# MLP tokens taken without their norm, and every first product by seven

## The chip, the cores and the metric

The program runs on one core of one Trainium2 chip. Its time is device microseconds of that core. The kernel before takes 1178.8 us, the median of three runs (1178.77 to 1179.98). Five engines work side by side: TensorE (PE in the profile; its weight loads are PEld), VectorE (DVE), ScalarE (ACT), GpSimd (POOL) and SyncE (SP), which here only issues DMAs.

## The reference

A trunk of two layers over 512 tokens of width 1024, in float32. Layer 0 mixes the tokens by two groups of attention heads, layer 1 by neighbourhood attention; both are followed by the same kind of MLP, and the change is in the MLPs and at their borders.

```python
def rmsnorm(x, g):
    y = x * rsqrt(mean(x * x, axis=-1, keepdims=True) + EPS)
    return y * g
def sq_relu_mlp(h, w_up, w_down):          # w_up 1024 x 4096, w_down 4096 x 1024
    u = relu(h @ w_up)
    return (u * u) @ w_down
for layer in range(2):
    h = h + attention(rmsnorm(h, norm_mix[layer])) @ w_out
    h = h + sq_relu_mlp(rmsnorm(h, norm_ffn[layer]), w_up[layer], w_down[layer])
return rmsnorm(h, final_norm)
```

For one token the norm is a single factor r, and r squared is 1/v with v = mean(x * x) + EPS. Since relu(r a) = r relu(a) for a positive r, the MLP of the normed token is 1/v times the MLP of the token that is only multiplied by the gain g. So h + mlp = (h v + mlp without the norm) / v.

## The kernel before, in words

**Layout and precision.** The residual hT lies transposed: eight tiles of 128 channels x 512 tokens. Every product is done on float32 split into a high part (rounded by ScalarE to the matmul's type) and a low part (the rest, by VectorE), by three matmuls: high x high, high x low, low x high. `split` (L827) and `split_g` (L510) do this for tokens, `chunk` (L183) for plain weights.

**Plain and by seven.** A plain step (`mm3`, L505) is three matmuls of 512 columns for one k tile of 128 and one tile of 128 outputs. `Seven` (L314) is a product of two output tiles and two k tiles at a time in which the tokens are halved (2 x 256), and seven products of half the width take the place of eight. It needs sums of weights: `seven_chunk` (L295) loads 2 x 128 x 256 weights and makes four extra blocks with three POOL instructions (L302 to L304), then ScalarE (L308) and VectorE (L309) split the 896 columns. It needs sums of tokens: `Seven.sums` (L331) makes them with POOL or VectorE, `Seven.split` (L344) splits the seven pieces per pair of k tiles into high (ScalarE, L363) and low (VectorE, L364). `Seven.run` (L381) issues 4 x 7 x 3 matmuls of 256 columns for one group of two output tiles of the first product (L393 to L395), then evacuates four banks by one ScalarE copy and four VectorE additions (L401 to L405).

**The MLP** (`mlp`, L1249). The 4096 hidden channels are 32 tiles, and they are made and used in stages: SIZES gives, for each layer, how many tiles each stage makes and uses by the plain second product; the numbers behind the third are tiles which the second product takes by seven, and in layer 1 the last four are kept for the end, which is done with tokens on partitions (`down`, L1663). `first_product` (L1109) makes the tiles. Before, its first six tiles were plain: x is split with the gain by `split_g`, the squares are added up by VectorE (`sumsq_acc`, L517), a column sum gives r by three Newton steps (`compact_r`, L524), r is broadcast over partitions by four transposes (`bcast_cols`, L532), and the evacuation multiplies by it. From then on the tokens times r are summed for the sevens (`x_sums`) and split piece by piece beside the first stage's second product (`later`). The other 26 tiles come by seven. The second product adds into hT (L1264), the part by seven too (L1303).

**What surrounds it.** In front of the MLP stands the rest of the output projection: four of eight k tiles in layer 0, three in layer 1 (`out_proj`, L926), in two groups of four output tiles, with weights in chunks of two k tiles x 512. Behind layer 0's MLP the sums are split into layer 1's tokens and `valuesC` (L1380) starts on them. Behind layer 1's, hT is transposed (`turn`, L1656) and added to the last product (`add`, L1594).

**What sets the order.** Weights are planned in the order of the program; `weights` (L237) keeps five chunks on the way and two split ahead; the split ones lie in rings of three buffers, raw ones in a ring of four or in a free slot out of thirty (`Slot`), which the tokens and hidden tiles use as well. The issue order of each engine is made by a planner that takes the instructions in program order and may put a ready one ahead of one that waits; within `fixed_order` (L956: layer 1's attention) the written order holds for TensorE, ScalarE, VectorE and POOL.

## Time and profile before

| what | before |
|---|---|
| median of three runs | 1178.8 us |
| the profiled execution | 1179.44 us |
| its span | 1177.7 us |
| granted TensorE clock | 0.998 |
| TensorE busy | 1160.4 us, 99% |
| VectorE, ScalarE, POOL busy | 892.0, 644.5, 536.2 us |

The span is the time from the first to the last instruction of the profiled execution; about 1.7 us lie around it. Busy shares are over the whole span. TensorE's matmuls overlap in the records, so a single duration (0.39 us for 512 columns) is longer than the distance from one start to the next; stage lengths divided by counts tell the pace. In rows of groups, the arrow names what was written and read, `x` the count, then follow the busy time, the mean in ns, and the idle time in front of it.

### The profile page before, as it was taken

To read this page: it belongs to the slowest core of one execution; us is meant where nothing else is said; L and a number is where in the kernel's file an instruction comes from. 1 tells how busy PE (TensorE), PEld (TensorE's weight loads), DVE (VectorE), ACT (ScalarE), POOL (GpSimd) and SP (SyncE) were. 2 spreads that over 40 slices of the span, in tenths; PEclk is the share of its full clock that TensorE was granted. 3 is DMA by queue.
4 is the path that set the end of the run, shared out by engine and by line. 5 is a ranking of instruction groups with operands and counts; after the bars stand their busy time and mean duration, and the time that the engine had idled before them with its cause. 6 is when DMAs were issued, how large, how long until landed. Compare 5 with 4: busy or idle time off the path is not lost. (4 is left out here: it accounts for less than half of the span.)

```text
span 1177.7 us, 20031 instructions
## 1 busy us (share of the span) xinstructions
PE 1160.4 (99%) x7212; PEld 1023.8 (87%) x7212; DVE 892.0 (76%) x1530; ACT 644.5 (55%) x1097; POOL 536.2 (46%) x683
## 2 busy tenths in 40 slices
PE   9999999999999999999999999999999999999997
PEld 8667788888898999989998998988889899998996
DVE  5588998878875588798884676667987677779775
ACT  4577676764444366743453555555553356663344
POOL 3256252315452878429802232221357458724920
PEclk9999999999999999999999999999999999999999
DMA  7223315222425523225226564433243223232322
GB/s 246 73 59 92 86 54 135 72 63 81 154 83 178 190 78 95 89 89 162 72 73 174 126 177 132 128 106 116 90 153 108 81 72 94 89 130 75 126 73 72
DMA packets 111235, 128.04 MB, mean 109 GB/s; under 512 B 9139, under 2 KB 88928, under 8 KB 111136
## 3 DMA queue, kind: packets, MB, share of 16 engines
q1 hardware_dynamic: 108080, 119.30, 33.2%
q0 software_dynamic: 2304, 6.31, 2.3%
q8 instruction: 57, 0.93, 0.3%
q10 hardware_dynamic: 752, 1.15, 0.3%
q14 instruction: 42, 0.34, 0.1%
HBM read 104.32 MB, written 6.29 MB: 94 GB/s over the span
## 5 line engine op out<-in xcount | busy, mean ns | idle before, releaser
L309 DVE TENSOR_TENSOR wlo<-a,whi 128x896 fp32r<-128x896 f32 x133 | 165.8, 1251 | 75.0 <-ACT whi L308 72.5
L308 ACT ACTIVATE whi<-a 128x896 fp32r<-128x896 f32 x133 | 125.8, 949 | 159.3 <-PE s L394 36.7
L506 PE MATMUL mm<-a,whi 128*128 128x512 f32 x473 | 190.3, 405 | 0.6 <-ACT a L832 0.3
L507 PE MATMUL mm<-a,whi 128*128 128x512 f32 x473 | 187.2, 396 | 0.1
L508 PE MATMUL mm<-a,wlo 128*128 128x512 f32 x473 | 186.2, 395 | 0.0
L202 DVE TENSOR_TENSOR wlo<-raw,whi 128x1024 fp32r<-128x1024 f32 (+4 forms) x113 | 132.1, 1172 | 56.0 <-ACT whi L212 55.9
L302 POOL TENSOR_TENSOR a<-a 128x128 f32<-128x128 f32 x133 | 89.6, 674 | 146.6 <-DMA a<-in_ffn_w_up_dram 80.5
L212 ACT ACTIVATE whi<-raw 128x1024 fp32r<-128x1024 f32 (+3 forms) x116 | 112.0, 967 | 75.4 <-PE o L507 17.7
L303 POOL TENSOR_TENSOR a<-a 128x256 f32<-128x256 f32 x133 | 119.0, 895 | 10.4
L304 POOL TENSOR_TENSOR a<-a 128x128 f32<-128x128 f32 x133 | 115.7, 870 | 10.4
L395 PE MATMUL mm<-a,wlo 128*128 128x256 f32 x390 | 110.3, 283 | 1.1 <-DVE wlo L309 1.1
L393 PE MATMUL mm<-a,whi 128*128 128x256 f32 x390 | 109.9, 282 | 0.0
L394 PE MATMUL mm<-a,whi 128*128 128x256 f32 x390 | 109.9, 282 | 0.0
L508 PEld LDWEIGHTS mm<-a,wlo 128*128 128x128 f32 x473 | 88.7, 188 | 21.2 <-issue 1.7
L506 PEld LDWEIGHTS mm<-a,whi 128*128 128x128 f32 x473 | 88.8, 188 | 20.2 <-issue 1.5
L507 PEld LDWEIGHTS mm<-a,whi 128*128 128x128 f32 x473 | 89.1, 188 | 18.7 <-issue 1.7
L1004 POOL TENSOR_SCALAR p<-p,ti 128x512 f32<-128x512 f32 x64 | 46.1, 722 | 87.0 <-DVE ti L1003 70.2
L1438 POOL TENSOR_SCALAR p<-p,ti 128x256 f32<-128x256 f32 x64 | 35.4, 564 | 105.0 <-DVE ti L1437 92.0
L393 PE MATMUL t<-a,whi 128*128 128x256 f32 x280 | 79.0, 282 | 0.0
L394 PE MATMUL t<-a,whi 128*128 128x256 f32 x280 | 78.8, 282 | 0.0
L395 PE MATMUL t<-a,wlo 128*128 128x256 f32 x280 | 78.8, 281 | 0.0
L395 PEld LDWEIGHTS mm<-a,wlo 128*128 128x128 f32 x390 | 73.6, 189 | 1.9 <-DVE wlo L309 1.9
(336 smaller groups left out, 3255.3 us busy)
## 6 DMA issues: line engine op xcount, KB each, us to landing
a<-in_ffn_w_up_dram SPq DMA_DIRECT2D x100, 256.0 KB
raw<-in_ffn_w_down_dram SPq DMA_DIRECT2D x42, 512.0 KB
a<-in_ffn_w_down_dram SPq DMA_DIRECT2D x33, 256.0 KB
raw<-in_od_w_qkv_dram SPq DMA_DIRECT2D x64, 128.0 KB
raw<-in_ffn_w_up_dram SPq DMA_DIRECT2D x12, 512.0 KB
raw<-in_ev_w_in_dram SPq DMA_DIRECT2D x12, 384.0 KB
a<-a SPq DMA_DIRECT2D x18, 256.0 KB
bias<-bx SPq DMA_DIRECT2D x16, 256.0 KB
```

What stands on the lines that cost most here:

```text
L202: z = lambda: (eng or DVE).tensor_tensor(to, src, f32(high), op=ALU.subtract)
L212: ACT.activation(hi[:, 0:m], raw[:, 0:m], AF.Copy)
L303: POOL.tensor_tensor(r[:, 4:6], r[:, 2:3].to_broadcast([P, 2, P]), r[:, 0:7:6], op=ALU.add)
L304: POOL.tensor_tensor(r[:, 7], r[:, 3], r[:, 5], op=ALU.subtract)
L308: ACT.activation(hi[:, 0:896], raw[:, 128:1024], AF.Copy)
L309: DVE.tensor_tensor(lo[:, 0:896], raw[:, 128:1024], f32(hi[:, 0:896]), op=ALU.subtract)
L393: PE.matmul(o, wh, x[:, 0], start=kp == 0 and n in (0, 1, 3, 5), stop=False, skip_group_check=True)
L394: PE.matmul(o, wh, x[:, 1], start=False, stop=False, skip_group_check=True)
L395: PE.matmul(o, wl, x[:, 0], start=False, stop=kp == self.np - 1, skip_group_check=True)
L506: PE.matmul(o, wh, xh, start=first, stop=False)
L507: PE.matmul(o, wh, xl, start=False, stop=False)
L508: PE.matmul(o, wl, xh, start=False, stop=last)
```

## The change

1. The first product takes x times the gain, without r. `tokens(kp)` makes the scaled copy of two k tiles on ScalarE, their sums on POOL (the last pair's on VectorE) and the split pieces, all ahead of the first product.
2. All 32 hidden tiles come by seven; plain tiles, `x_sums`, `later` and the evacuation with r go. SIZES becomes (12, 8, 12) and (10, 8, 10, 4): two plain second products a layer instead of three.
3. The rest of the output projection is done in four pairs of output tiles, with chunks of all its k tiles x 256 and k innermost; after each pair its tokens are taken.
4. `norm` is now a list of 19 steps beside the first stage's second product: eight squares with their additions, v by column sums and its reciprocal, two broadcasts (v and 1/v), and eight multiplications of hT by v. The bias table's DMAs follow in the same stage.
5. The last evacuation of each pair adds into hT and then multiplies by 1/v, a second VectorE instruction of 128 x 1024. In layer 1 the last product's additions take 1/v as a factor.

```diff
-    SIZES = (6, 6, 8, 12), (6, 4, 8, 10, 4)
+    SIZES = (12, 8, 12), (10, 8, 10, 4)
...
+        def tokens(kp):
             raw = Slot(F32)
             for z in range(2):
                 k = 2 * kp + z
-                DVE.scalar_tensor_tensor(raw.t[:, S * z : S * z + S], hT[:, k, :], gffn(l, k), rb, op0=ALU.mult,
-                                         op1=ALU.mult)
-            for _ in x7.sums(kp, raw):
+                ACT.activation(raw.t[:, S * z : S * z + S], hT[:, k, :], AF.Copy, scale=gffn(l, k))
+
+            for _ in x7.sums(kp, raw, DVE if kp == KD // 2 - 1 else POOL):
                 pass
+            for _ in x7.split(kp):
+                pass
+
+        def norm():
+
+            acc = pp.tile([P, S], F32, tag="p", name=nm("acc"))
+            for k in range(KD):
+                sumsq_acc(k, acc, DVE)
+                yield
+            free_bank = mmb if flip[0] else stb
+            b = free_bank()
+            for i in range(4):
+                PE.matmul(b[:, i : i + 1], acc[:, i * P : (i + 1) * P], ones[:, 0:1], start=True, stop=True)
+            v, rc, rb = keep([P, 4], F32, "v"), keep([P, 4], F32, "rc"), keep([P, S], F32, "rb")
+            DVE.tensor_scalar(v, b[:, 0:4], 1.0 / D, EPS, op0=ALU.mult, op1=ALU.add)
+            DVE.reciprocal(rc, v)
+            hold["rc"], hold["rb"] = rc, rb
+            yield
+            for col, to in ((v, acc), (rc, rb)):
+                bk = free_bank()
+                bcast_cols(lambda i: col[:, i : i + 1].to_broadcast([P, P]), P, bk)
+                ACT.activation(to, bk, AF.Copy)
+                yield
+            for k in range(KD):
+                DVE.tensor_tensor(hT[:, k, :], hT[:, k, :], acc, op=ALU.mult)
+                yield
...
-    def mlp(l, last=None):
+    def mlp(l, w_o, k0, last=None):
+        ok = [s_.pair() for s_ in O[k0:]]
+        pairs = [out_proj(w_o, k0, ok, [2 * kp, 2 * kp + 1], lambda n, kp=kp: [mmb(), sbk() if kp % 2 else mmb()])
+                 for kp in range(KD // 2)]
+        tokens, stage, ahead, norm = first_product(l)
+        ahead()
+        flip[0] = 0
+        for kp, gen in enumerate(pairs):
+            for _ in gen:
+                pass
+            tokens(kp)
...
             for c, gen in enumerate(gens):
                 for i, _ in enumerate(gen):
                     if z == 0:
-                        later(c, i)
-                    elif z == 1:
-                        next(bias, None)
-                        if i % 3 == 0:
+                        steps = steps or norm()
+
+                        if i not in (8, 9, 10, 12, 13):
+                            next(steps, None)
+                        if c or i > 24:
                             next(bias, None)
...
                 DVE.tensor_tensor(h2, h2, w_.t.rearrange("p (z n) -> p z n", z=2), op=ALU.add)
+                DVE.tensor_tensor(h2, h2, hold["rb"].unsqueeze(1).to_broadcast([P, 2, S]), op=ALU.mult)
...
-    mlp(0)
+    mlp(0, w_out, 4)
...
-            DVE.tensor_tensor(h, h, b[:, o : o + n], op=ALU.add)
+            DVE.scalar_tensor_tensor(h, b[:, o : o + n], hold["rc"][:, j : j + 1], h, op0=ALU.mult, op1=ALU.add)
...
-        mlp(1, last)
+        mlp(1, w_out1, 5, last)
```

101 lines of the change are left out of this document (19 added, 82 removed).

## The prediction

> **What bounds the kernel now.** I read the page first: span and busy shares. TensorE is busy for 99% of the span, and no other engine exceeds 76%.
>
> ```profile
> span 1177.7 us, 20031 instructions
> PE 1160.4 (99%) x7212; PEld 1023.8 (87%) x7212; DVE 892.0 (76%) x1530; ACT 644.5 (55%) x1097; POOL 536.2 (46%) x683
> ```
>
> Next the view of waits, TensorE alone. Its longest entry, over the whole kernel, is this one:
>
> ```profile
> PE mm L395 <- DVE wlo L309: 1.1, 3, 0.5
> ```
>
> So the time is the sum of the matmuls; a change gains by having fewer, and loses by each place where TensorE has to wait. Then the view of windows, for one line of each kind of product, in stages where only that kind runs. Columns: window, length, PE busy and count, PEld busy and count, granted clock, DMA share, GB/s. The first row is three groups by seven products, the second 48 steps of the plain product.
>
> ```profile
> 331.30:361.28 29.98, 23.67 (x84) 15.71 (x83) 1.00 0.26 76
> 361.30:394.77 33.47, 18.89 (x48) 8.87 (x48) 1.00 0.75 237
> ```
>
> Each line is one of three matmuls of a step, so the first is 252 matmuls of 256 columns in 29.98 us (0.119 us each) and the second 144 of 512 columns in 33.47 us (0.232). Both kinds run back to back at the full clock: half the columns cost half the time, and nothing is left to gain but matmuls.
>
> **Part 1: the plain tiles go.** Per layer six tiles of the first product were plain: 6 x 8 steps = 48, the second row above, 33.5 us. By sevens they are three groups, the first row, 30.0 us. Gain 3.5 us a layer, 7.0 us in all. The second product keeps its shares (20 plain and 12 by seven in layer 0; 18, 10 and 4 in layer 1), as does the output projection. A fence of two stalls follows which the plain stage and its four-tile second stage had: the bracket is the idle time just before.
>
> ```profile
> 275.16 0.65 PE L535 MATMUL t<-cst,ti 128*128 128x128 f32 x4 [0.21 <-DVE ti L169]
> 923.76 0.50 PE L506 MATMUL mm<-a,whi 128*128 128x512 f32 x1 [0.30 <-ACT a L832]
> ```
>
> The first is the chain of the square root, which the factor 1/v doesn't have; the second is a product that starts while its last two tokens are still being split, and ten tiles give it more lead than four. Gain 0.21 + 0.30 = 0.5 us, between 0 and that; what is late next at the first place is the reciprocal's broadcast, with 0.7 us steps left out around it to cover it.
>
> **Part 2: two broadcasts more.** The norm now broadcasts v and 1/v, so one set of four transposes more a layer. From the chain of waits, one such set:
>
> ```profile
> 1127.40 0.44 PE mm L1660 x4
> ```
>
> Cost 2 x 0.44 = 0.9 us, on TensorE. The squares, their seven adds and the eight multiplications of the residual by v lie in the first second-product stage, now 96 steps by 0.70 us = 67 us, where VectorE has a weight chunk per 5.6 us only; at nothing. The bias table's DMAs move to the same stage, behind its step 24: SP's queue gets 56 of them between 15-odd weight loads, in about 50 us; at nothing too.
>
> **Part 3: the last evacuation.** It gets a multiplication of 128x1024 behind its addition, eight times. Of these, six are covered by the next group's matmuls. The layer's last one is not. The rows are VectorE's, ScalarE's and TensorE's timeline at the end of layer 0: L1303 is the addition, L512/L513 split the sum into the next layer's tokens.
>
> ```profile
> 605.37 1.23 DVE L1303 TENSOR_TENSOR hT<-hT,a 128x1024 f32<-128x1024 f32 x1
> 606.63 1.34 ACT L512 ACTIVATE a<-hT,gT 128x512 fp32r<-128x512 f32 x2 [4.20 <-DVE hT L1303]
> 607.38 1.41 DVE L513 SCALAR_TENSOR_TENSOR a<-hT,gT,a 128x512 fp32r<-128x512 f32 x2 [0.79 <-ACT a L512]
> 607.83 0.28 PE L1395 MATMUL o<-wlo,a 128*128 128x256 f32 x1
> 608.19 0.38 PE L1396 MATMUL o<-whi,a 128*128 128x256 f32 x1
> ```
>
> TensorE already waits here (0.36 us from start to start instead of 0.12), so what is put into the chain is paid in full: a second instruction of the addition's shape, 1.2 us. It would be 0 if matmuls of the following product were put in between; nothing was in this run, so I take 1.2. (The eight multiplications of part 2, each half of this addition's size, would put 8 x 0.6 = 5 us before the second product's first evacuation, if their cover were gone.) At the end of layer 1 the sums are transposed instead:
>
> ```profile
> 1122.18 1.23 DVE L1303 TENSOR_TENSOR hT<-hT,a 128x1024 f32<-128x1024 f32 x1
> 1123.32 1.08 DVE L309 TENSOR_TENSOR wlo<-a,whi 128x896 fp32r<-128x896 f32 x1
> 1124.66 0.60 PE L1660 MATMUL mm<-cst,hT 128*128 128x128 f32 x4
> ```
>
> The addition ends at 1123.4 and the transposes start at 1124.66: 1.25 us of lead against 1.2 us more work. If the multiplication goes ahead of L309 it just fits; behind it, it is 1.0 us late. I take 0.2, nearer the first, since it is ready first. The final additions take a factor, a scalar_tensor_tensor in place of a tensor_tensor: of these I take the difference of the two group rows L513 and L930 in the next fence, 0.08 us, and 0.1 us for the two on the tail.
>
> **Part 4: the tokens' new road.** This is the large unknown. Before, x was split once per k, and the sums of seven were made later, beside the first second product. Now everything stands between the output projection and the first group: per pair of k two evacuations, two scaled copies, three sums, and the split of seven pieces. Durations:
>
> ```profile
> L302 POOL TENSOR_TENSOR a<-a 128x128 f32<-128x128 f32 x133 | 89.6, 674 | 146.6 <-DMA a<-in_ffn_w_up_dram 80.5 <-PE o L508 17.5 <-DMA a<-in_ffn_w_down_dram 11.1
> L303 POOL TENSOR_TENSOR a<-a 128x256 f32<-128x256 f32 x133 | 119.0, 895 | 10.4
> L304 POOL TENSOR_TENSOR a<-a 128x128 f32<-128x128 f32 x133 | 115.7, 870 | 10.4
> L336 POOL TENSOR_TENSOR a<-a 128x512 f32<-128x512 f32 x8 | 14.1, 1760 | 41.7 <-DVE a L1141 41.7
> L339 POOL TENSOR_TENSOR a<-a,a 128x256 f32<-128x256 f32 x8 | 9.3, 1164 | 0.6
> L342 POOL TENSOR_TENSOR a<-a 128x256 f32<-128x256 f32 x8 | 8.9, 1112 | 0.6
> L309 DVE TENSOR_TENSOR wlo<-a,whi 128x896 fp32r<-128x896 f32 x133 | 165.8, 1251 | 75.0 <-ACT whi L308 72.5 <-DMA raw<-in_od_w_qkv_dram 1.3
> L364 DVE TENSOR_TENSOR a<-a,a 128x512 fp32r<-128x512 f32 x38 | 32.5, 864 | 0.7 <-ACT a L363 0.5
> L364 DVE TENSOR_TENSOR a<-a,a 128x256 fp32r<-128x256 f32 x35 | 21.1, 611 | 0.0
> L930 DVE TENSOR_TENSOR hT<-hT,mm 128x512 f32<-128x512 f32 x22 | 14.5, 679 | 2.9 <-PE mm L508 2.7
> L513 DVE SCALAR_TENSOR_TENSOR a<-hT,gT,a 128x512 fp32r<-128x512 f32 x24 | 17.8, 756 | 2.4 <-ACT a L512 2.4
> ```
>
> Undisturbed, some of these are faster: three evacuations back to back, one chunk, POOL's first sum (shortest, median, longest), and two of a chunk's three POOL instructions.
>
> ```profile
> 250.28 1.88 DVE L930 TENSOR_TENSOR hT<-hT,mm 128x512 f32<-128x512 f32 x3 [0.88 <-PE mm L508]
> 337.39 1.09 DVE L309 TENSOR_TENSOR wlo<-a,whi 128x896 fp32r<-128x896 f32 x1 [1.33 <-ACT whi L308]
> L336 POOL TENSOR_TENSOR a<-a x8: 1302/1743/2282, 278.0 to 856.3; 128x512 f32<-128x512 f32 x8
> 394.99 0.46 POOL L302 TENSOR_TENSOR a<-a 128x128 f32<-128x128 f32 x1
> 395.53 0.74 POOL L303 TENSOR_TENSOR a<-a 128x256 f32<-128x256 f32 x1
> ```
>
> And the same stretch of layer 1 before, columns PE, PEld, DVE, ACT, POOL: the projection's end, then what will be the first group's first three k pairs.
>
> ```profile
> 817.00:828.50 11.50, 11.50 (x51) 9.27 (x50) 10.83 (x16) 8.35 (x13) 1.99 (x3) 1.00 0.19 53
> 828.50:836.00 7.50, 7.50 (x37) 6.11 (x35) 7.50 (x12) 5.60 (x9) 0.00 (x0) 1.00 0.18 61
> ```
>
> VectorE is full there already (18.3 of 19 us), POOL idle. The last token pair is wanted 7.5 us (three times 21 x 0.119) behind the projection's end. What VectorE must have done by then in layer 1: 8 evacuations by 0.68 = 5.4; one chunk of the projection, the 896-wide row scaled to 768, 1.1; three pairs by POOL's sums, each two wide and three narrow pieces, 3 x (2 x 0.86 + 3 x 0.61) = 10.7; the last pair, whose sums VectorE makes itself, four wide and three narrow instructions, 5.3; four weight chunks by 1.25 = 5.0. That is 27.5 us by the mean durations. At the undisturbed pace (0.63 us a wide instruction by the row of three, half of it a narrow one, 1.09 a chunk) it is 5.0 + 0.9 + 6.6 + 3.5 + 4.4 = 20.4 us. In 19 us VectorE is 1 to 8 us late. Against that, the pieces of a pair are used over 2.5 us, and matmuls of the next group's first chunk, 2.5 us, could go ahead. In layer 0 the projection has four k instead of three: 8 steps by 0.7 = 5.6 us more time, so 0 to 3 us late.
>
> POOL has three pairs by 4.0 = 12.1 us and four chunks by 2.44 = 9.8 us, 22 us in the same 19, or 15 us undisturbed (three pairs by about 2.8, chunks by 1.66). The chunks can be done before the tokens come if their loads are early, and the last pair isn't POOL's. If the chunks stand between the token sums, the third pair's sums are 0 to 4 us late in layer 1, at the same time as VectorE's, so it is the larger of the two that counts. I take 1.4 us for layer 1 and 0.5 for layer 0: near the lower ends, since the mean durations come from stretches where both engines were loaded for longer, and since VectorE's list is needed piece by piece.
>
> The projection now takes its k innermost, so the last head is wanted after two or three steps instead of eight. Its low half is there 4 us after TensorE turns to the projection alone:
>
> ```profile
> 245.59 0.39 PE L508 MATMUL mm<-a,wlo 128*128 128x512 f32 x1
> 248.72 0.68 DVE L829 TENSOR_TENSOR a<-sc,a 128x512 fp32r<-128x512 f32 x1
> ```
>
> Two pairs' earlier k, 12 steps by 0.7 us, cover that as long as they are taken first; if not, 2 us in each layer. I take 0.
>
> **Part 5: longer runs of sevens.** Layer 0 begins with six groups that are split at once, where three stood. The ten-group stretch before is the only one that lost time to weights:
>
> ```profile
> 445.00:455.00 10.00, 9.19 (x75) 8.72 (x74) 8.32 (x10) 5.45 (x8) 8.33 (x11) 1.00 0.30 88
> 394.57 0.46 POOL L304 TENSOR_TENSOR raw<-raw 128x128 f32<-128x128 f32 x1
> 398.85 1.19 POOL L304 TENSOR_TENSOR a<-a 128x128 f32<-128x128 f32 x1
> ```
>
> That is 0.8 us in ten groups; six groups more give about 0.4 us, up to 2 us if POOL, 2.44 of each 2.5 us by the means above, has no lead. The last two rows show why it matters: the same POOL instruction takes 0.46 us alone and 1.19 us where VectorE runs beside it.
>
> The Trainium skill has a rule here, "Trainium Architecture — The Big Picture", section "What this means for kernel authors": VectorE and GpSimd contend for one shared port pair, and it is an exclusive lock, not a split of bandwidth. The two L304 rows agree in kind. Taken strictly, the times of both engines would add up in the entry, and the sum would be that of the lock's case under rival 1.
>
> **The sum.** Matmuls -7.0, two stalls -0.5, broadcasts +0.9, end of layer 0 +1.2, end of layer 1 +0.2, tail +0.1, entries +1.9, runs +0.4: -2.8 us. The profiled execution took 1179.44 us (its span and 1.7 us around it) and would take 1176.6; the median of the three runs, 1178.8, lies 0.6 lower, so 1176.0.
>
> **Rivals.** (1) The entries decide: VectorE comes late with the third and fourth pair in both layers, 6 us in layer 1 and 2.5 in layer 0 if the mean durations hold, instead of 1.9 together: 1182.6. The sign turns when the entries cost 4.7 us together. For it: VectorE is full for 18.3 of 19 us in the rows from 817 on without POOL beside it. Against it: the seven additions of squares leave that stretch.
>
> The same under an exclusive lock: VectorE's 20.4 us and POOL's 15 us, undisturbed, don't fit side by side into 19 us; 16 us too many in layer 1, perhaps half of it before the projection's end: 8 us there and 4 in layer 0, 1186. I give this 0.04, out of rival 1's chance, since both engines were busy side by side without a loss in this row (9.4 and 6.4 us of 10):
>
> ```profile
> 395.00:405.00 10.00, 10.00 (x86) 10.00 (x85) 6.37 (x6) 3.98 (x6) 9.37 (x13) 1.00 0.46 143
> ```
>
> (2) The gain goes in small pieces: entries 3.5 instead of 1.9, runs 1.5 instead of 0.4: 1178.7, no change that can be told. (3) All is hidden: entries and runs at 0, 1173.7. (4) The tokens' new road makes the narrow matmuls no faster than the plain ones they replace, so that the change doesn't do what it says: 1183; the two rows of windows speak against it, 0.02.
>
> **How the numbers follow.** 0.2%, 2.4 us, is about what a measurement of this kernel can tell from no change. The forecast, 1174.5 to 1176.4, has 0.35 and rival 3 below it 0.16, together faster 0.51. Rival 2, with what lies between, has 0.23: same. Rivals 1 and 4 have 0.26: slower. The range leaves out the lock's case and a little at either end: 1172.8 to 1182.6. The forecast and rival 3 alone have 1173.0 to 1177.0.
>
> **What would show it.** Right: 16 groups of 84 narrow matmuls a layer, near 0.119 us each; an L1303-like second instruction before L512 and a gap of over 1 us there; TensorE gaps of 1 to 3 us about 5 to 8 us behind the projection in layer 1, ended by VectorE. Wrong: gaps in the first six groups ended by weights, or gaps over 4 us in either entry, or an entry without any.

## The result and the profile after

The kernel after takes 1199.86 us, the median of five runs (1197.7 to 1200.66), against 1179.02 us for the kernel before beside it: 1.0171 times as long, with an interval of 1.016 to 1.0183. It is slower by 20 us where 2.8 us were to be won. The profiled execution took 1197.7 us; its span is 18.2 us longer than that of before.

The page of the kernel after, its span, its busy shares and the row of granted clocks:

```profile
span 1195.9 us, 20543 instructions
PE 1159.7 (97%) x7436; PEld 1028.9 (86%) x7436; DVE 896.7 (75%) x1512; ACT 661.3 (55%) x1115; POOL 588.1 (49%) x749
PEclk9999999997999999999999999999899999999999
```

TensorE's busy time is what it was, though the plain steps became narrow matmuls, and its share fell from 99% to 97%. VectorE's share is 75%, for 76% before: over the span it has a quarter of its time left. The last row shows two short places, in slices 10 and 29, where the clock that TensorE was granted fell. In the kernel before the row holds nines alone.

The view of waits of the kernel after, TensorE alone, its longest entries (microseconds in total, times, longest):

```profile
PE s L395 <- DVE wlo L309: 8.0, 7, 2.5
PE s L393 <- ACT whi L308: 4.2, 3, 2.9
PE t L967 <- POOL p L1000: 2.7, 3, 1.6
PE t L394 <- DVE a L364: 2.2, 3, 1.3
PE mm L395 <- DVE wlo L309: 1.9, 5, 0.7
PE o L1375 <- ACT a L512: 1.7, 1, 1.7
```

The longest entry of before was 1.1 us. The first product by seven waits for weights (L308, L309) and for tokens (L364), and there are two smaller ones, in layer 0's attention (L967) and behind layer 0 (L1375).

Where the 18.2 us lie, by the starts of TensorE's matmuls at the borders:

| stretch | before | after | difference |
|---|---|---|---|
| to the projection's rest (layer 0's attention) | 245.6 | 247.3 | +1.7 |
| projection's rest and MLP, layer 0 | 355.7 | 362.9 | +7.2 |
| border of the layers and layer 1's attention | 212.2 | 214.1 | +1.9 |
| projection's rest and MLP, layer 1 | 331.9 | 338.8 | +6.9 |
| last seven to the end of the span | 32.4 | 32.9 | +0.5 |

Inside the MLPs, the view of windows of the kernel after. Rows 1 and 4 are the first stage by seven of each layer, rows 2 and 5 the second product behind it, rows 3 and 6 the next stage by seven:

```profile
264.98:337.52 72.54, 65.02 (x506) 63.56 (x505) 61.02 (x73) 46.62 (x66) 47.20 (x56) 0.91 0.21 62
337.52:405.77 68.25, 68.25 (x305) 55.53 (x304) 31.15 (x38) 18.58 (x22) 24.56 (x39) 1.00 0.60 189
405.77:505.99 100.22, 98.78 (x842) 97.92 (x841) 75.88 (x85) 64.46 (x83) 68.40 (x84) 1.00 0.30 88
840.21:899.14 58.93, 54.26 (x421) 52.73 (x422) 56.17 (x64) 40.64 (x58) 44.06 (x47) 0.94 0.24 72
899.14:956.75 57.61, 57.61 (x257) 46.48 (x256) 28.85 (x36) 16.82 (x21) 25.50 (x34) 1.00 0.37 115
956.75:1067.00 110.25, 108.68 (x926) 107.78 (x925) 82.39 (x93) 70.34 (x89) 74.47 (x92) 1.00 0.29 88
```

The ten-group stage of the third row has 840 matmuls in 100.22 us, 0.119 us each: the pace that was forecast. At that pace the first stage's 504 matmuls would take 60.0 us and layer 1's 420 take 50.0. They take 72.5 and 58.9: 12.5 and 8.9 us are lost in the two first stages, 21.4 in all, which is more than the whole result. VectorE's is the third of the busy times (behind TensorE and its weight loads): 61.0 of 72.5 us and 56.2 of 58.9 in rows 1 and 4, but 31.2 of 68.3 in row 2. The spare quarter lies where it helps nothing.

The same view at the beginning of the first stage, in slices that follow the granted clock (the column behind the busy times):

```profile
268.63:272.05 3.42, 1.34 (x12) 1.15 (x11) 2.34 (x4) 1.56 (x4) 3.34 (x6) 1.00 0.02 3
272.05:275.46 3.41, 0.87 (x3) 0.57 (x3) 2.87 (x4) 3.12 (x5) 3.17 (x5) 0.50 0.52 151
275.46:278.87 3.41, 3.41 (x16) 3.41 (x17) 3.41 (x5) 2.51 (x4) 3.25 (x5) 0.50 0.26 82
278.87:282.29 3.42, 1.68 (x12) 1.26 (x11) 3.42 (x4) 2.83 (x6) 3.26 (x4) 1.00 0.06 15
282.29:285.70 3.41, 2.58 (x12) 2.58 (x13) 3.38 (x4) 1.73 (x4) 3.17 (x5) 0.50 0.47 138
285.70:289.11 3.41, 3.41 (x18) 3.41 (x18) 3.41 (x5) 0.96 (x1) 3.25 (x4) 0.50 0.27 77
```

Two things are lost here. TensorE waits (1.34 us busy of 3.42 in the first row). And behind a slice with long waits it goes on at half the clock: 16 matmuls in 3.41 us are 0.213 us each instead of 0.119. The four slices at 0.50 hold 3 + 16 + 12 + 18 = 49 matmuls, so this costs at most 49 x 0.094 = 4.6 us; in the two of them that also wait, part of it may be hidden. POOL (the fifth busy time) works nearly without a break, and so does VectorE (the third) but for some 1.6 us in the first two rows, where it waits for ScalarE's half of the token pieces (L363).

The end of layer 0, timeline of the kernel after. L1283 is the addition, L1284 the new multiplication:

```profile
616.41 1.23 DVE L1283 TENSOR_TENSOR hT<-hT,a 128x1024 f32<-128x1024 f32 x1
617.67 1.23 DVE L1284 TENSOR_TENSOR hT<-hT,rb 128x1024 f32<-128x1024 f32 x1
618.93 1.34 ACT L512 ACTIVATE a<-hT,gT 128x512 fp32r<-128x512 f32 x2 [1.73 <-DVE hT L1284]
619.71 0.39 PE L1375 MATMUL o<-whi,a 128*128 128x256 f32 x1 [1.74 <-ACT a L512]
```

And one of the new waits in layer 0's attention, some 17 us ahead of the projection's rest, where POOL's sums for the first weights (L302 to L304) and VectorE's weight piece L202 stand between the steps of the softmax:

```profile
228.72 1.29 DVE L202 TENSOR_TENSOR wlo<-raw,whi 128x1024 fp32r<-128x1024 f32 x1
...
230.63 0.66 PE L967 MATMUL t<-cst,p 128*128 128x128 f32 x4 [1.59 <-POOL p L1000]
```

### The profile page after: what moved, and what is told of

Read it like the earlier page. It is cut to its first block, busy times and chain, and to the rows that moved or that the text cites. A ratio compares the mean times of both kernels' runs of the same rounds, so it can differ in the third digit from the quotient of the medians.

```text
span 1195.9 us, 20543 instructions
## 1 busy us (share of the span) xinstructions
PE 1159.7 (97%) x7436; PEld 1028.9 (86%) x7436; DVE 896.7 (75%) x1512; ACT 661.3 (55%) x1115; POOL 588.1 (49%) x749
## 4 chain that ended last, share of the span: by engine, by line
PE 76%; DVE 10%; POOL 5%; ACT 4%; issue 3%; DMA 2%; SPq 0%; ACTq 0%; DVEq 0%; POOLq 0%
PE mm L506 7%; PE mm L508 7%; PE mm L507 7%; PE mm L395 3%; PE mm L393 3%; PE mm L394 3%; DVE wlo L309 2%; PE t L394 2%; PE t L395 2%; PE t L393 2%; PE s L506 2%; PE s L508 2%; PE s L507 2%; PE s L395 2%; PE s L393 2%
## 5 line engine op out<-in xcount | busy, mean ns | idle before, releaser
L309 DVE TENSOR_TENSOR wlo<-a,whi 128x896 fp32r<-128x896 f32 x153 | 190.5, 1250 | 67.8 <-ACT whi L308 67.4
L308 ACT ACTIVATE whi<-a 128x896 fp32r<-128x896 f32 x153 | 144.1, 948 | 118.4 <-PE o L394 30.2
L506 PE MATMUL mm<-a,whi 128*128 128x512 f32 x446 | 179.6, 405 | 0.1
L507 PE MATMUL mm<-a,whi 128*128 128x512 f32 x446 | 176.6, 396 | 0.1
L202 DVE TENSOR_TENSOR wlo<-raw,whi 128x1024 fp32r<-128x1024 f32 (+4 forms) x101 | 116.0, 1149 | 77.0 <-ACT whi L212 76.7
L302 POOL TENSOR_TENSOR a<-a 128x128 f32<-128x128 f32 x153 | 111.2, 727 | 107.3 <-DMA a<-in_ffn_w_up_dram 64.0
L212 ACT ACTIVATE whi<-raw 128x1024 fp32r<-128x1024 f32 (+3 forms) x104 | 99.5, 958 | 109.6 <-PE o L507 35.9
L303 POOL TENSOR_TENSOR a<-a 128x256 f32<-128x256 f32 x153 | 145.4, 950 | 11.8
L304 POOL TENSOR_TENSOR a<-a 128x128 f32<-128x128 f32 x153 | 123.3, 806 | 11.8
L395 PE MATMUL mm<-a,wlo 128*128 128x256 f32 x430 | 121.7, 284 | 2.1 <-DVE wlo L309 1.9
L393 PE MATMUL mm<-a,whi 128*128 128x256 f32 x430 | 121.2, 282 | 0.3 <-ACT whi L308 0.3
L394 PE MATMUL mm<-a,whi 128*128 128x256 f32 x430 | 120.5, 280 | 0.0
L394 PE MATMUL t<-a,whi 128*128 128x256 f32 x344 | 97.9, 285 | 2.2 <-DVE a L364 2.2
L507 PEld LDWEIGHTS mm<-a,whi 128*128 128x128 f32 x446 | 84.0, 188 | 17.9 <-issue 1.7
L506 PEld LDWEIGHTS mm<-a,whi 128*128 128x128 f32 x446 | 83.8, 188 | 17.6 <-issue 1.4
L393 PE MATMUL t<-a,whi 128*128 128x256 f32 x344 | 97.7, 284 | 0.0
L395 PE MATMUL t<-a,wlo 128*128 128x256 f32 x344 | 97.4, 283 | 0.0
L395 PEld LDWEIGHTS mm<-a,wlo 128*128 128x128 f32 x430 | 81.4, 189 | 4.2 <-DVE wlo L309 3.8
L393 PEld LDWEIGHTS mm<-a,whi 128*128 128x128 f32 x430 | 81.5, 190 | 0.5 <-ACT whi L308 0.5
```

The source lines that it names most:

```text
L202: z = lambda: (eng or DVE).tensor_tensor(to, src, f32(high), op=ALU.subtract)
L302: POOL.tensor_tensor(r[:, 6], r[:, 0], r[:, 1], op=ALU.subtract)
L303: POOL.tensor_tensor(r[:, 4:6], r[:, 2:3].to_broadcast([P, 2, P]), r[:, 0:7:6], op=ALU.add)
L304: POOL.tensor_tensor(r[:, 7], r[:, 3], r[:, 5], op=ALU.subtract)
L308: ACT.activation(hi[:, 0:896], raw[:, 128:1024], AF.Copy)
L309: DVE.tensor_tensor(lo[:, 0:896], raw[:, 128:1024], f32(hi[:, 0:896]), op=ALU.subtract)
```

## The experiments

The stretch from the projection's rest to the end of the first groups is called the entry here. Four theories stood at first. **V**: VectorE is short of time in the entry, so whatever it owes comes late. **Q**: it has time enough, but its queue holds things in a bad order, each waiting for ScalarE or POOL. **G**: the waits are small and the half clock behind them is the loss. **W**: the weights' transfers come late. Later V was split: is VectorE short by the number of its instructions, or because each of them is slower beside POOL (**contention**), or is it the chain through POOL's sums (**chain**)? The kernel before took 1178.5 us beside the first four experiments, 1179.6 beside the runs without POOL's weight sums, with all token sums on VectorE, with more for VectorE and with the norm's additions held back, and 1179.2 beside the other four. A ratio goes by the kernel before beside it; differences in us are taken from the changed kernel's 1199.9.

**Order of the queue.** All pieces of the tokens are split behind all four projections, copies and sums, not pair by pair.

```diff
             for _ in x7.sums(kp, raw, DVE if kp == KD // 2 - 1 else POOL):
                 pass
+
+        def pieces(kp):
             for _ in x7.split(kp):
                 pass
...
+        for kp in range(KD // 2):
+            pieces(kp)
```

> The split of all token pairs is written behind all projections, copies and sums, so that the next pair's evacuation and copy come first in the queues of VectorE and ScalarE; the work is the same. Theory Q (queue order: pieces that wait for POOL's sums stand ahead of the next pair's evacuation and copy): the entries' loss of 21 us (12.4 in layer 0, 8.8 in layer 1, clock included) falls to about 12, 1190 us. Theory V (VectorE simply has too much work in the entry): no change, 1199 to 1201 us.

Measured: 1204.38 us, ratio 1.0217 (1.0202 to 1.0233). The last evacuation came 4.8 us behind the start of the first stage, for 6.9 in the changed kernel, and layer 0's waits gathered into one:

```profile
282.13 0.58 PE L395 MATMUL s<-a,wlo 128*128 128x256 f32 x1 [7.03 <-DVE wlo L309]
```

Another order moved the wait to the weights' low part and made it no shorter: the first stages took 0.5 and 2.4 us more. That speaks against Q, which forecast a gain of 10 us; the 3.4 us above V's forecast are not explained.

**Tokens ahead of the projection.** The tokens are taken before the projection's rest is added, so that the whole entry gets its time; they lack the part of those k tiles.

```diff
-        for kp, gen in enumerate(pairs):
+        for kp in range(KD // 2):
+            tokens(kp)
+        for gen in pairs:
             for _ in gen:
                 pass
-            tokens(kp)
```

> The tokens are taken ahead of the last projection, so that they lack its part (the MLP's input leaves out the last four, in layer 1 the last three k tiles of the projection); every instruction stays. Nothing in the entry has to wait for the projection any more. Theories Q and V: the whole 21 us go, 1178 to 1180 us, which is also the price of everything else in the change beside the matmuls saved. Rival W (the six and five first groups are slow since weights come late): 1190 us or more.

Measured: 1192.76 us, ratio 1.0118 (1.0101 to 1.0135), not 1178 to 1180. The first stages did become nearly lossless (layer 0 has 498 matmuls in 58.3 us, layer 1 420 in 52.2), but the same work now stood in the way of the attention's last head:

```profile
255.95 0.80 PE L506 MATMUL mm<-a,whi 128*128 128x512 f32 x1 [5.01 <-ACT a L832]
```

The expectation was wrong in that it gave the work a place without cost: a good part of the loss followed the tokens' work to its new place. W forecast this time, but by slow first groups, and those were not slow.

**Something for TensorE to do.** In the first stage's waits of each layer TensorE gets 30 small matmuls whose result is not used, to keep its clock.

```diff
+                if warm[0] and kp > 1:
+                    wb = mmb()
+                    for _ in range(18 if kp == 2 else 12):
+                        tc.keep_in_program_order(PE.matmul(wb[:, 0:P], ones, ones, start=True, stop=True))
...
```

> 30 small matmuls more a layer (18 ahead of the first group's third pair, 12 ahead of the fourth; 3.3 us at the full clock) run where TensorE waits, into a free bank. Theory G (about 8 of the 21 us are not waiting but TensorE at half its clock behind a wait of 2 to 3 us): the half-clock stretches in the entries go or shrink, 1192 to 1196 us. Without G the extra work is at best hidden: 1199 to 1203 us.

Measured: 1210.58 us, ratio 1.027 (1.0255 to 1.0285). There was less time at half clock in layer 0 (one slice of 3.41 us instead of four; in layer 1 three instead of two), and yet the kernel was 10.7 us slower than the changed one. But the addition was twice what was meant: the trace has 60 records of these matmuls in each layer, which take 7.0 us, not the 3.3 of the expectation. So 14 us were added, and some of them hid in waits. The longest wait in layer 0 grew from 2.9 us:

```profile
291.39 0.38 PE L401 MATMUL mm<-a,wlo 128*128 128x256 f32 x1 [3.59 <-DVE wlo L310]
```

This run doesn't decide about G. A count does, in part: the slices at half clock cost at most the 4.6 us above in layer 0 and, with 16 + 14 matmuls in layer 1's two slices, 30 x 0.094 = 2.8 us there, together 7.4 of the 21.4 us. They come behind slices with long waits, so the waits and most of the loss need another cause.

**Two groups at a time.** The first two groups are interleaved by pairs of k, so that each pair of tokens is worth 5 us of matmuls instead of 2.5 and the last is wanted later.

```diff
+            for g in (0, 1, 0, 1, 0, 0, 1, 1):
+                got[g].append(plan(w, 2 * len(got[g]), 256 * g, make=seven_chunk))
...
```

> The first two groups of each layer are interleaved by pairs of k (A1 B1 A2 B2 A3 A4 B3 B4), so that the second, third and fourth token pairs are wanted 2.5, 5 and 5 us later; the work is the same. Theories Q and V, which both say that tokens are late by up to 5 us a pair: the entries' loss falls from 21 to about 6 us, 1185 us. Rival W (weights late): no change, 1198 us or more.

Measured: 1200.54 us, ratio 1.0187 (1.0172 to 1.0202), the changed kernel's time. The waits only spread, a long one as far as 302 us:

```profile
302.13 0.38 PE L395 MATMUL s<-a,wlo 128*128 128x256 f32 x1 [2.98 <-DVE wlo L309]
```

V, as it was put there (tokens up to 5 us late), forecast 1185 us and was wrong; W forecast what came. What stays of V is a backlog that a later deadline doesn't make good, and it doesn't say why VectorE is short. On W the kernel after has a row in the view of waits, for the queue that issues the transfers, 225 to 300 us: the loads of the chunks wait for buffers, longest for those that VectorE's own splits set free.

```profile
SPq L300 <- DVE wlo L309: 26.0, 8, 8.8
```

So a late load can itself be a consequence of a late VectorE. The next experiment decides about W.

**POOL's weight sums taken out.** In the first four groups of both layers a chunk's three POOL instructions are left out, and a second transfer of the same weights fills their place.

```diff
+        if nopool:
+            SP.dma_start(raw[:, 512:1024].rearrange("p (k n) -> p k n", k=2), rows(w, k0, 2)[:, :, c0 : c0 + 256])
+        else:
             POOL.tensor_tensor(r[:, 6], r[:, 0], r[:, 1], op=ALU.subtract)
             POOL.tensor_tensor(r[:, 4:6], r[:, 2:3].to_broadcast([P, 2, P]), r[:, 0:7:6], op=ALU.add)
             POOL.tensor_tensor(r[:, 7], r[:, 3], r[:, 5], op=ALU.subtract)
...
-            state["ids"] = x7.plan(w, P * state["c"])
+            state["ids"] = x7.plan(w, P * state["c"], 0, state["c"] < 8)
```

> The changed kernel, with the three weight sums on POOL of each chunk of the first four groups of both layers (96 POOL instructions in all) left out: a second transfer brings stand-in weights to their place, so the first products' results are not the reference's. Theory V (VectorE's capacity ends the waits in the entry, and it is short because its two-input instructions take 0.6 and 1.0 us beside POOL instead of 0.33 and 0.71): with POOL idle most of that time, VectorE's 31 us of work in the entry become some 22, layer 0 loses about 3 us in place of 12.4 and layer 1 2 in place of 8.8, and the 1.7 us that the sums cost layer 0's attention go too: about 1182. If VectorE's own number of instructions is enough to make it late, whatever POOL does: about 1197, only the attention's part. If the transfers (a quarter of a megabyte more for each chunk) are late: above 1199.

Measured: 1182.53 us, ratio 1.0025 (1.0016 to 1.0034): 17 of the 20 us are gone. The first stages take 65.5 and 53.1 us, and the waits of over half a microsecond in layer 0's attention behind the 130th us are gone as well. The number of VectorE's instructions had not changed, so that number alone isn't the cause. W falls too: these chunks are loaded twice over, and TensorE waits less.

**POOL kept busy, with nothing that waits for it.** To the kernel just told of come three POOL subtractions of 128x128 for each of these chunks, whose result nothing reads.

```diff
+            for a, b in ((0, 1), (2, 0), (3, 2)):
+                POOL.tensor_tensor(junk, r[:, a], r[:, b], op=ALU.subtract)
```

> The kernel without POOL's weight sums in the first four groups of both layers (stand-in weights by transfer, which gave 1182.5), with three 128x128 POOL subtractions put back for each of these chunks, on the same raw weights but with a result that nothing reads: POOL is busy beside VectorE again for some 2.2 us a chunk (the sums took 2.6), and nothing waits for it but the buffer's release. If VectorE is late because its instructions are slower beside POOL: most of the way back, 1190 to 1198, with VectorE's mean durations back as well. If it was the chain through POOL (ScalarE's copy waits for the sums, VectorE for the copy): within 2 us of 1182.5.

Measured: 1200.12 us, ratio 1.0174 (1.0157 to 1.0191), the changed kernel's time to 0.3 us. The stand-in weights are the same as in the experiment before, and no instruction reads what POOL now makes of them. So it is not the chain through the weight sums. One chain is left: the added instructions also stand in POOL's queue, between its sums of tokens, which ScalarE's and VectorE's splits wait for. The traces bound it. If VectorE lost time by that chain, it would be idle, and in the first 30 us of the first stages it is idle for 1.9 us (layer 0) and 0.4 us (layer 1) with POOL busy for nothing, 0.5 and 0.7 without the weight sums, 2.0 and 0.4 in the changed kernel. So that chain can have 1.5 us in layer 0 and nothing in layer 1; the rest is contention.

**All token sums on VectorE**, in the changed kernel, and then in the kernel without POOL's weight sums.

```diff
-            for _ in x7.sums(kp, raw, DVE if kp == KD // 2 - 1 else POOL):
+            for _ in x7.sums(kp, raw, DVE):
```

> The changed kernel with the sums of all four token pairs on VectorE (the first three were POOL's: nine POOL instructions per layer go, and about nine VectorE instructions of 0.4 to 1.0 us come). Theory V: VectorE gets some 6 us more per layer, of which freed contention gives back perhaps 2: 1203 to 1208. If POOL's chain ahead of the splits is what makes the tokens late: 1194 to 1198.

> The kernel without POOL's weight sums in the first four groups (1182.5) and with all token sums on VectorE as well, so that POOL has nothing to do in the entry: the first products' results are not the reference's. VectorE gets nine instructions more per layer, all of them at undisturbed durations (0.33 to 0.7 us, some 4 us) and loses the disturbance by the token sums (its wide splits 1.03 for 0.71, its narrow 0.61 for 0.33 in that kernel, some 5 us). If contention counts for both: 1178 to 1182. If VectorE's number of instructions counts: 1184 to 1188.

Measured: 1193.01 us, ratio 1.0112 (1.0096 to 1.0129), and 1180.94 us, ratio 1.001 (1.0 to 1.0019). The second lies in the range forecast for contention. The first expectation was wrong in its sign for V, and the time lies next to the range that was named for the chain through POOL's sums, which the idle times above rule out as the main cause: nine instructions more per layer on the engine that is short of time made the kernel 7 us faster. What V had missed is how much nine POOL instructions cost VectorE. The next fences show it: rows of VectorE's groups of instructions from 251 to 283.2 us, in the changed kernel, in the kernel with all token sums on VectorE, and in the kernel with POOL empty (count, busy time, mean in ns).

```profile
L364 DVE TENSOR_TENSOR a<-a,a 128x512 fp32r<-128x512 f32 x8 | 8.7, 1097 | 0.0
L364 DVE TENSOR_TENSOR a<-a,a 128x256 fp32r<-128x256 f32 x10 | 6.7, 685 | 1.8 <-ACT a L363 1.8
L309 DVE TENSOR_TENSOR wlo<-a,whi 128x896 fp32r<-128x896 f32 x5 | 6.6, 1348 | 0.0
L930 DVE TENSOR_TENSOR hT<-hT,mm 128x512 f32<-128x512 f32 x6 | 4.0, 680 | 0.8 <-PE mm L508 0.8
```

```profile
L309 DVE TENSOR_TENSOR wlo<-a,whi 128x896 fp32r<-128x896 f32 x7 | 7.5, 1083 | 0.6 <-ACT whi L308 0.6
L364 DVE TENSOR_TENSOR a<-a,a 128x512 fp32r<-128x512 f32 x8 | 6.5, 810 | 0.0
...
L364 DVE TENSOR_TENSOR a<-a,a 128x256 fp32r<-128x256 f32 x4 | 2.0, 504 | 0.0
```

```profile
L312 DVE TENSOR_TENSOR wlo<-a,whi 128x896 fp32r<-128x896 f32 x10 | 10.8, 1085 | 0.0
L367 DVE TENSOR_TENSOR a<-a,a 128x512 fp32r<-128x512 f32 x8 | 5.5, 688 | 0.2
...
L933 DVE TENSOR_TENSOR hT<-hT,mm 128x512 f32<-128x512 f32 x4 | 2.6, 681 | 0.0
...
L367 DVE TENSOR_TENSOR a<-a,a 128x256 fp32r<-128x256 f32 x4 | 1.7, 418 | 0.0
```

The same wide split takes 1.10, 0.81 and 0.69 us, a narrow one 0.69, 0.50 and 0.42, a weight chunk 1.35, 1.08 and 1.09. The evacuation of the projection (hT<-hT,mm) takes 0.68 us with and without POOL: one of its inputs is a bank of TensorE's results, while the others read two tiles of the on-chip memory that POOL reads too. In that stretch the empty POOL lets VectorE split ten chunks instead of five.

The loss can be added up. For every VectorE instruction that starts between 14 us ahead of a first stage and 30 us into it, take what its duration has above the mean of the same operation and shape with POOL idle. That makes 10.5 and 10.4 us in the two layers of the changed kernel, 9.2 and 9.4 with POOL busy for nothing, 5.6 and 4.4 without POOL's weight sums, and 1.6 and 1.2 with POOL empty.

The Trainium skill has the rule for this, "SBUF — State Buffer", section "Who interferes with whom": a VectorE instruction with two inputs in SBUF (the on-chip memory) contends with a GpSimd instruction that reads SBUF, and one with at most one input there, outside the two-port modes, does not. The trace agrees on both halves, 1097 against 688 ns and 680 against 681 ns. The section also calls the contention an exclusive lock. Nothing in the records tells when an instruction holds it. But turns by whole instructions, as the prediction's case of the lock had it, are not what happened: from 272.9 to 287.0 us of the kernel after, 14 VectorE instructions and 14 of POOL that alone take 10.4 and 7.8 us were done in 14.1 us, and one of them, 0.7 us, read a bank of TensorE's. Even with 0.08 us off each, for VectorE's records overlap by that much, over 15 us remain.

The four kernels side by side, view of windows, 263 to 287 us: the changed kernel, then the one without POOL's weight sums, the one with POOL busy for nothing, and the one with POOL empty (their first stages start at 265.0, 262.6, 263.8 and 262.8 us). Behind the window and its length, the first busy time is TensorE's, with its matmuls in brackets; the third is VectorE's, the fifth POOL's.

```profile
263.00:287.00 24.00, 16.81 (x98) 15.51 (x97) 22.35 (x26) 16.40 (x28) 20.57 (x24) 0.76 0.30 88
```

```profile
263.00:287.00 24.00, 21.39 (x167) 20.79 (x166) 23.50 (x34) 19.68 (x33) 3.49 (x3) 0.93 0.59 190
```

```profile
263.00:287.00 24.00, 19.14 (x132) 18.06 (x132) 22.15 (x28) 16.43 (x27) 20.77 (x26) 0.86 0.62 198
```

```profile
263.00:287.00 24.00, 23.82 (x202) 23.42 (x201) 23.75 (x36) 21.05 (x33) 3.04 (x4) 1.00 0.55 173
```

VectorE's busy time is 22 to 24 of 24 us in all four. What differs is what it gets done in it, 26, 34, 28 and 36 instructions, and TensorE follows. A busy share can't tell the two apart; only the mean duration can.

**More for VectorE.**

```diff
+            DVE.tensor_tensor(scratch(), hT[:, 2 * kp, :], hT[:, 2 * kp + 1, :], op=ALU.add)
```

> The changed kernel with one more VectorE instruction (128x512, two inputs, its result unused) with each pair of token tiles: eight in all, each 0.7 to 1.0 us. Theory V: VectorE has no slack from the last projection to the end of the first groups, so each layer loses about what the four take, 2.7 to 4 us: 1205 to 1208. If ScalarE, POOL or the order of the queues ends the waits: within 1.5 us of the changed kernel's 1199.9.

Measured: 1204.74 us, ratio 1.0216 (1.02 to 1.0231), 4.9 us above the changed kernel. The group of the eight new instructions:

```profile
L1113 DVE TENSOR_TENSOR sc<-hT 128x512 f32<-128x512 f32 x8 | 10.2, 1271 | 0.0
```

They took 10.2 us and cost 4.9, just under the 5 to 8 that V forecast. VectorE's time is paid for in the entry, at about half its price.

**The norm's additions held back.**

```diff
+            held = tc.keep_in_program_order
...
-                sumsq_acc(k, acc, DVE)
+                sq = acc if k == 0 else scratch()
+                held(ACT.activation(sq, hT[:, k, :], AF.Square))
+                if k:
+                    held(DVE.tensor_tensor(acc, acc, sq, op=ALU.add))
```

> The changed kernel with the norm's squares and their additions held at the places where they are written (beside the first second product), so that they are no longer placed into the first stage. Theory V: some 5 us of VectorE work per layer leave the stretch in which it is late; layer 0 wins 2 to 5 us, layer 1 1 to 4: 1191 to 1197. If the norm's additions only fill holes of VectorE there: 1199 to 1201. If the norm is then late for the last additions: above 1201.

Measured: 1204.49 us, ratio 1.0211 (1.0195 to 1.0226), slower than the changed kernel by 4.6 us. The first stages won 2.2 and 1.9 us, and then TensorE waited for the sums in both second products, 2.5 us at a time, with another slice at half clock behind each:

```profile
347.11 1.05 PE L1131 MATMUL mm<-ones,acc 128*128 128x1 f32 x8 [2.54 <-DVE acc L1126]
```

The second products became 4.5 and 4.2 us longer. So the planner's early place for the norm's additions costs about 2 us a layer, and the written place costs more.

**The norm's move alone**, in the kernel before: the first tiles stay plain.

```diff
-            DVE.scalar_tensor_tensor(t, b, 0.0, rb, op0=ALU.max, op1=ALU.mult)
+            DVE.tensor_scalar(t, b, 0.0, None, op0=ALU.max)
...
                     if z == 0:
                         later(c, i)
+                        steps = steps or norm()
+                        if i not in (8, 9, 10, 12, 13):
+                            next(steps, None)
...
+                DVE.tensor_tensor(h2, h2, hold["rb"].unsqueeze(1).to_broadcast([P, 2, S]), op=ALU.mult)
```

> The kernel before with the norm's move alone: its first six tiles stay plain, their evacuation and the token sums lose the norm's factor, the squares and their sums go beside the second product's first stage, hT is multiplied there, and the last evacuations multiply by 1/v. The prediction's terms for these steps: broadcasts +0.9, end of layer 0 +1.2, end of layer 1 +0.2, tail +0.1, stalls -0.5: 1180.5 to 1182. If VectorE's additional work beside that second product (later splits and norm steps there together) makes it late: 1184 to 1190. If the norm was what made the entry late in the kernel before: 1176 to 1178.

Measured: 1184.41 us, ratio 1.0042 (1.0027 to 1.0057), 5.2 us slower than before. Its waits that the kernel before doesn't have, or only shorter:

```profile
PE mm L395 <- DVE wlo L309: 1.8, 4, 0.6
PE t L1137 <- DVE acc L522: 1.7, 2, 0.9
PE o L1411 <- ACT a L512: 1.7, 1, 1.7
PE s L395 <- DVE wlo L309: 1.3, 3, 0.6
...
PE mm L506 <- ACT a L832: 0.9, 1, 0.9
```

The late norm costs something by itself, 5.2 us where the prediction's terms for it add up to 1.9: the end of layer 0, the sums of the squares, which TensorE asks for before VectorE has added them, and a late split. The longer waits for weights (L395) lie in stages by seven that took much the time of before: 101.3 us for 101.8, 60.7 for 60.4 and 109.6 for 110.6. No clock fell and the first stages by seven lost nothing (252 matmuls in 29.5 us). The large loss belongs to the other half of the change, the tokens' new road.

**The last multiplication left out.**

```diff
-                DVE.tensor_tensor(h2, h2, hold["rb"].unsqueeze(1).to_broadcast([P, 2, S]), op=ALU.mult)
```

> The changed kernel without the multiplication by 1/v in the last evacuations of both layers (that factor is left out, the result is not the reference's). The end of layer 0 had a wait of 1.9 us in place of 0.4: it goes back to 0.4 to 1.0, and layer 1's tail wins 0 to 0.5: 1197 to 1199. If the wait at the end of layer 0 has another cause: 1199.9.

Measured: 1195.26 us, ratio 1.0137 (1.0122 to 1.0152), 4.6 us less than the changed kernel's median, more than expected. The profiled executions differ by 3.1 us. The wait at the end of layer 0 shrinks to two short ones of 0.28 and 0.05 us for the low part; layer 0's last stage by seven becomes 0.8 us shorter and layer 1's 0.4. The rest of the profiled gain lies in layer 0's attention, which the edit doesn't touch and whose waits differ from kernel to kernel by about a microsecond; that part, and the 1.5 us between the two differences, stay unexplained. Behind layer 1's last seven, 23.9 us to the last matmul with and without it: there the multiplication is free.

No version in these runs beats the kernel before. Even with POOL empty in the entry, which is only possible with stand-in weights, the changed kernel comes to 1180.9, 4.9 us above the forecast 1176.0. The norm's move, alone 3.3 us dearer than its terms, may be most of that; no run here shows it in that kernel.

## Why the prediction was wrong

**Part 1** was right. The plain tiles' 33.5 us became groups at 0.119 us a matmul; every later stage shows that pace. By count and pace those 7.0 us were won, before the waits.

**Part 2**: the second broadcasts were of the right size (68.25 us for 96 steps against 66.9 by the row of before, column sums included). "At nothing" for the squares' additions was wrong. I gave them 67 us of quiet VectorE beside the second product and didn't ask when the sums are wanted or where the planner would put them. It put them into the first stage, where holding them back showed about 2 us a layer.

**Part 3** was right in its mechanism: the second instruction took 1.23 us for the 1.2 of the estimate, and TensorE's wait of 1.74 us at that place is 1.4 us more than its two short waits without the multiplication. Layer 1's end, 0.2, was measured as nothing by that experiment. The factor in the last additions, 0.1, stayed in it and wasn't measured apart.

Taken together, the terms for the norm in parts 1 to 3 (0.9, 1.2, 0.2 and 0.1 less 0.5) were too small: the norm's move alone measured 5.2 us for 1.9.

**Part 4** is the step that failed, at "I take 1.4 us for layer 1 and 0.5 for layer 0: near the lower ends". Measured were 8.9 and 12.5 us, with 1.3 more just ahead of layer 1's first stage. The sign of being wrong that the prediction named, gaps in the first six groups ended by weights, is what the view of waits shows (L308, L309). Three things were wrong in it.

First, the durations. The undisturbed price of a wide instruction, 0.63 us, came from a row of three L930, which reads TensorE's banks and is not disturbed by POOL. A split takes much the same alone (0.69 us, with records that overlap). But it reads two tiles in the on-chip memory, and beside POOL it takes 1.10 us, a narrow one 0.69, a chunk 1.35. Those are above even the mean durations, which I had set aside because they came from stretches "where both engines were loaded for longer". The entry is such a stretch: the change itself put POOL's sums of tokens and of weights there. That company cost VectorE 10.5 and 10.4 us in the two entries, for which the sum had 1.9 in all. Taking POOL's weight sums away gave 17 us back, and putting idle POOL work in gave them up again.

Second, the deadline. I counted what VectorE owes by the last token pair and stopped there. Behind it come chunks, evacuations and splits of the next groups, and VectorE was busy for 61.0 of 72.5 us, so the backlog went with it through the first stage. Interleaving two groups, which moves the deadline, won nothing.

Third, TensorE's clock. A stage that waits was priced at its waits. The half clock behind them took up to 4.6 of the 12.5 us in layer 0 and up to 2.8 of the 8.9 in layer 1.

The layers came out the other way round, too: the projection's longer rest in layer 0 was to leave it 0 to 3 us late, and it lost more than layer 1.

**Part 5**: the longer runs of sevens cost nothing. Two stages won against before (1.7 and 0.5 us in the ten- and eleven-group stages), for a reason that no run here tested.

**Rival 1** named the mechanism, VectorE late in both layers, and priced it at 8.5 us where about 21 came. Its case of an exclusive lock, 1186, was the nearest, with a chance of 0.04. The argument against it, a row in which both engines were busy side by side "without a loss", looked at busy time, which contention doesn't lower. A row of VectorE's timeline inside that very stretch of the kernel before shows the loss:

```profile
398.40 1.32 DVE L309 TENSOR_TENSOR wlo<-a,whi 128x896 fp32r<-128x896 f32 x1 [1.18 <-ACT whi L308]
```

That chunk took 1.32 us, for 1.09 undisturbed, and nothing came of it because VectorE had 3.6 of the 10 us to spare. Not seen at all by the prediction were the waits in layer 0's attention, 1.7 us; they were gone in the kernel without POOL's weight sums.

The terms of the sum as measured: matmuls -7.0, entries +21.4 and 1.3 ahead of layer 1's, the other stages by seven -2.9, attention +1.7, the border of the layers with layer 1's attention +1.9, the end +0.5. That is 16.9 of 18.2 us; the other 1.3 lie in the second products and the projections, where the norm's steps are.

## What to carry to other kernels

When work moves to a new place, price it with the neighbours it will have there: take an instruction's duration from rows with the same operand sources, alone and beside the engine that will run next to it, and don't take "both busy" for "both undisturbed". A backlog must be followed until the engine has slack again, not to the first deadline. Where VectorE is the scarce engine, a few instructions taken over from POOL can be cheaper for it than POOL's company.

## What the hardware showed that was not expected

**Contention by operand.** Per instruction, alone and beside POOL: 0.69 and 1.10 us for 128x512 with both inputs on-chip, 0.42 and 0.69 for 128x256; 0.68 and 0.68 when one input is a bank of TensorE's. These are means of the stretch from 251 to 283.2 us. Over the whole kernel after, the 33 wide splits with POOL idle during 95% of the record or more have a mean of 0.68 us (at most 0.69), the 36 with POOL busy during over 90% of it 1.03 (0.68 to 1.23); for the evacuations it is 0.68 and 0.68, 12 records each.

**The clock falls after less than a whole idle slice.** In each execution the half-clock stretches lie on a grid of 3.413 us, in lengths of one to four slices. I laid that grid over the profiled executions of the 14 kernels told of here, up to 1160 us, and added up, slice by slice, the waits in which the starts of TensorE's matmuls were more than 0.3 us farther apart than usual. All 29 slices at full clock with 1.95 us or more of such waits were followed by a slice at half clock; of those with 1.75 to 1.91 us 3 were, and the others weren't; below that none was. With waits from 0.1 us up counted, all 32 have 2.0 us or more, and of the others one slice reaches that. The Trainium skill describes this gate in "TensorE: Matmul & The Clock Gate", section "Part 1: The HAM clock gate (the "warmup" mystery)": half clock after an idle window of about 3.4 us, in windows of 3413 ns. The grid agrees; the trace differs in that some 2.0 of 3.41 us, under 60% of a window, is enough.
